# Summing the partial rows of a modulation vector with a ones column, two steps later, in a two-layer hybrid decoder trunk

## Chip, cores, metric

The kernel runs on 1 core of a Trainium2 chip. The metric is device time in microseconds (us) of one execution.

## What is computed

Two layers act on x (512 tokens by 1024). Each layer first makes six modulation vectors of 1024 from the condition c; they scale and shift the two norms and gate the two residual updates. Only the following of the reference matters here:

```python
mod = jax.nn.silu(c) @ ada_w + ada_b                     # (1, 6 * 1024) per layer
sh_m, sc_m, gt_m, sh_f, sc_f, gt_f = jnp.split(mod[:, None, :], 6, axis=-1)
h = rms_norm(x, norm_mix) * (1 + sc_m) + sh_m
...                                                       # input projection and three token mixers
x = x + gt_m * (jnp.concatenate([o_a, o_b, o_c], axis=-1) @ w_out)
h = rms_norm(x, norm_ffn) * (1 + sc_f) + sh_f
gate, up = jnp.split(h @ w_gate_up, 2, axis=-1)
x = x + gt_f * ((jax.nn.silu(gate) * up) @ w_down)
```

## The kernel before, in words

x is kept transposed, as eight tiles `x0` to `x7` of 128 features by 512 tokens. Every large product is taken with both operands split into a high and a low part (`whi`, `wlo` for weights, `hh`, `hl` for the normed activations, `fh`, `fl` for the FFN's), three matmuls for each pair of tiles. `mm` (L298) is the helper that issues every matmul that is not a transpose. In the FFN the products are `pg` (gate), `pu` (up) and `pd` (down); in the mixers `pj`, `pvt` and others. The weights come over SyncE's queue into `wraw` (L570, two buffers, 1 MB each), ScalarE makes the high part (L581), VectorE (sometimes GpSimd) the low part (L582).

The modulation vectors are made by the generator `ada` in halves of 512 columns: 2 layers, 6 vectors, 2 halves, 24 half vectors. The 1024 rows of `ada_w` are eight blocks of 128 partitions. One block is scaled by the column of silu(c) that belongs to it and added to the running sum `acc` of 128 partitions by 512 columns; VectorE does both in one instruction (L413, L415), or ScalarE scales (L417, L420) and GpSimd adds (L418). So when the eight blocks are in, `acc` holds 128 partial rows, and these have to be summed over the partitions, with the result turned from a row of 512 into 4 columns of 128, because `mods[l]` keeps features on partitions.

The end of a half vector does that (L428 and the lines behind it): four transposes of 128 by 128 on TensorE write one PSUM bank `pada` of the two with tag `tp` (L435), VectorE reduces the bank along the free dimension to 4 columns of `mods` (L436) and adds the bias (L437). For the two scale vectors one more small VectorE instruction (L441) makes `na`, the norm's factor.

At the start four half vectors are run one after the other with whole tiles of 4 blocks (the vectors with m of 0 and 1 of layer 0), since the first norm needs them. The other 20 half vectors are side work: `ada` yields after every step of two blocks (tiles `araw2`, which rotate through the three tags `ab0` to `ab2` and show as `araw` in the trace), and the main work calls `next(side)` between its own pieces, in layer 0's mixers (8 half vectors) and in layer 0's FFN (12, those of layer 1). `chain` strings them together; `run` drains a generator.

The order of the instructions on each engine isn't that of the program text: the tile framework schedules the whole program by a timeline of its own, with the priorities that the text sets. A change in one place can so move instructions elsewhere.

Of the kernel before, what the change touches and what calls it, by code (L numbers as in the profile page):

```python
# [227 lines left out]
def trunk(ctx, tc, I, out, dbg=None):  # L228
# [79 lines left out]

    # ---------------- constants and per-layer vectors
    cst = cp.tile([128, CONST_AT["eye16"][0]], F32, name="cst")  # L310
# [50 lines left out]
    V.memset(mhalf, -0.5)  # L361
    V.memset(onesd, 1.0 / D)

    def turn_vrows(l, n=113):
# [12 lines left out]

    # ---------------- modulation: one of the six vectors of a layer
    def ada_raw():
# [4 lines left out]

    pend = [] if "v" in ORDER else [first_vrows]

    def ada(l, m, halves=(0, 1), tile_=ada_raw, eng=G):
        for half in halves:
# [4 lines left out]
            while k < NK:  # L393
                raw = tile_()
                nk = raw.shape[1]
                nc.sync.dma_start(raw, I["ada_w"][l, k * 128:(k + nk) * 128, c0:c0 + 512]
                                  .rearrange("(k p) c -> p k c", p=128))
                for kk in range(nk):
                    t = raw[:, kk]
                    if eng is T:  # L400
                        if k == 0:
                            acc = P("gd", "prow")
                        mm(acc[0:1], scol[:, k:k + 1], t, start=(k == 0), stop=(k == NK - 1))
                        k += 1
                        continue
                    if tile_ is ada_raw:
                        if k == 0:
                            acc = S2("acc")
                        o = acc
                    else:  # L410
                        o = t
                    if eng is V and k:
                        V.scalar_tensor_tensor(o, t, scol[:, k:k + 1], acc, op0=OP.mult, op1=OP.add)  # L413
                    elif eng is V:
                        V.tensor_scalar(o, t, scol[:, 0:1], None, op0=OP.mult)  # L415
                    elif k:
                        A.activation(t, t, AF.Copy, scale=scol[:, k:k + 1])  # L417
                        G.tensor_tensor(o, t, acc, op=OP.add)  # L418
                    else:
                        A.activation(o, t, AF.Copy, scale=scol[:, 0:1])  # L420
                    acc = o
                    k += 1
                if pend:
                    pend.pop()()
                yield
            p = P("tp", "pada")
            if eng is T:
# [5 lines left out]
            else:  # L433
                for j in range(4):
                    T.transpose(p[:, j * 128:j * 128 + 128], acc[:, j * 128:j * 128 + 128], ident)  # L435
                V.tensor_reduce(mods[l][:, c:c + 4], view4(p), axis=AX.X, op=OP.add)  # L436
                V.tensor_add(mods[l][:, c:c + 4], mods[l][:, c:c + 4], vcol[l][:, 16 + c:20 + c])  # L437
            if m in (1, 4):
# [5 lines left out]
    def run(g):  # L444
        for _ in g:
            pass

    # ---------------- norm and split, by halves of the tokens
    HALF = (slice(0, 256), slice(256, 512), slice(0, 512))
# [115 lines left out]
    marks.extend(norm.last)  # L565
    # ---------------- weights: raw pieces and their two parts
    def raw_piece(w, r0, nk, c0, n):
# [43 lines left out]
    def halves(ms, tile_, then, n):  # L611
        for m in ms:
            tile_(0, m)
        after = then(0)
        for j, m in enumerate(ms):
            tile_(1, m)
            for _ in range(n if j else 1):
                next(after, None)
# [7 lines left out]
    def layer(l, side, norm, vt):  # L626
# [8 lines left out]

        # ---- values and gates, token major
        wt = vt if vt is not None else vt_weights(l)
# [15 lines left out]
        if l == 0 and KN["lt"] == 1:  # L653
            with behind(KN["ga"] & 4):
                late()
        # ---- GDN gates
        with prio("gate"):
# [36 lines left out]

        # ---- positions of the compressed blocks
        pe = small("pe", 128, 1)
# [6 lines left out]

        # ---- GDN projections, short convolution
        ckv = {n: c8.tile([128, NH, S], F32, tag=n, name=n) for n in ("ck", "cq", "cv", "cz")}
# [39 lines left out]

        # ---- GDN: norms, token major k
        ck, cq, cv, cz = ckv["ck"], ckv["cq"], ckv["cv"], ckv["cz"]
# [33 lines left out]

        # ---- GDN: decay, (I + A)^T and q k^T of each chunk, keys on partitions
        with prio("dec"):
# [37 lines left out]

        # ---- GDN: inverse of I + A; 32 x 32 blocks in lanes, then two doublings
        with prio("inv"):
# [78 lines left out]

        # ---- GDN: the chunks in turn
        def gdn_out(c):
# [75 lines left out]

        # ---- attention projections
        def rope(p, dst):
# [49 lines left out]

        # ---- compressed keys and values
        w2 = c8.tile([128, 2, 3, 64], F32, tag="w2", name="w2")
# [62 lines left out]

        # ---- attention over keys at or before the query
        def weights_t(pts, nkb):
# [122 lines left out]

        # ---- output projection
        w_out = I["w_out"][l]
# [100 lines left out]
    def chain(*gens):  # L1325
        for g in gens:
            yield from g

    # ---------------- final norm, token major
    def last(norm, i):  # L1330
# [68 lines left out]
```

## Time and profile before

| | |
|---|---|
| median of 3 runs | 1460.61 us (1457.11 to 1462.02) |
| profiled execution, span from first to last instruction | 1460.0 us |
| TensorE matmuls busy, share of the span | 1381.5 us, 95% |
| VectorE busy | 861.2 us, 59% |
| ScalarE busy | 643.6 us, 44% |
| GpSimd busy | 358.9 us, 25% |
| mean granted clock of TensorE, share of full | 0.972 |
| moved from HBM | 168 MB |

The profiled execution shows its span and no other time of its own; the median of the runs is 0.6 us above it. Times in the trace count from the start of the span. The stages follow each other: start to about 60 us, mixers of layer 0 to 392, FFN of layer 0 to 764, mixers of layer 1 to 1092, FFN of layer 1 to the end. A matmul's duration in the trace is its latency, and matmuls overlap: what one costs the stream is the step from its start to the next one's start. Busy PE therefore isn't PE at its peak. PEld is the load of the stationary operand.

### The profile page before, as it was taken

How to read it: one execution, taken by the hardware profiler on the slowest of the kernel's cores; microseconds unless marked ns; L12 is line 12 of the kernel's file. 1: busy time of each engine (PE TensorE's matmuls, PEld its weight loads, DVE VectorE, ACT ScalarE, POOL GpSimd, SP SyncE). 2: the span in 40 equal slices, each digit the busy share in tenths (PEclk: the TensorE clock that was granted, in tenths of full speed). 3: DMA queues.
4: the chain of work that ended last, by engine and by line, in shares of the span. 5: the costliest groups of instructions: out<-in, count | busy, mean ns of one | idle time of the engine just before them, and what ended most of it. 6: DMA issues, size and time to landing. Idle time of an engine off the chain costs nothing.

```text
span 1460.0 us, 21266 instructions
## 1 busy us (share of the span) xinstructions
PE 1381.5 (95%) x8357; PEld 1152.6 (79%) x8357; DVE 861.2 (59%) x1600; ACT 643.6 (44%) x1174; POOL 358.9 (25%) x325
## 2 busy tenths in 40 slices
PE   3789989999999999999999999999999999999997
PEld 3667867787977888788898887778788888888887
DVE  6866877875655555446466576788554343343434
ACT  4567536665543432342254463667443322222231
POOL 4556541344431410140042024124340000000000
PEclk7899999999999999999999999989999999999999
DMA  9646554002056654465441223400212332232231
GB/s 324 220 157 217 152 178 130 4 1 87 30 184 223 193 165 158 131 188 186 125 127 30 87 63 105 145 30 1 82 36 89 101 113 87 87 116 87 87 116 58
DMA packets 137160, 171.47 MB, mean 117 GB/s; under 512 B 14778, under 2 KB 95332, under 8 KB 136932
## 3 DMA queue, kind: packets, MB, share of 16 engines
q1 hardware_dynamic: 137060, 170.11, 36.2%
q8 instruction: 65, 1.06, 0.3%
q14 instruction: 35, 0.29, 0.1%
HBM read 168.00 MB, written 2.10 MB: 117 GB/s over the span
## 4 chain that ended last, share of the span: by engine, by line
PE 78%; DVE 7%; DMA 7%; POOL 3%; ACT 3%; issue 2%; SPq 0%; POOLq 0%; DVEq 0%; ACTq 0%
PE pd L298 16%; PE pg L298 15%; PE pu L298 15%; PE pj L298 11%; DMA araw<-in_ada_w_dram 5%; PE pw L298 3%; PE psc L298 2%; PE pwc L298 2%; PE pob L298 2%; PE ppt L1106 2%; POOL araw L418 2%; PE pvt L298 1%; DVE araw L413 1%; PE pkk L298 1%; DVE wlo L582 1%
## 5 line engine op out<-in xcount | busy, mean ns | idle before, releaser
L581 ACT ACTIVATE whi<-wraw 128x1024 fp32r<-128x1024 f32 (+1 forms) x181 | 187.6, 1038 | 469.2 <-PE pd L298 130.6
L582 DVE TENSOR_TENSOR wlo<-wraw,whi 128x1024 fp32r<-128x1024 f32 (+1 forms) x171 | 218.2, 1276 | 175.3 <-ACT whi L581 169.9
L298 PE MATMUL pj<-hh,whi 128*128 128x512 f32 (+1 forms) x376 | 148.0, 395 | 7.8 <-DVE cacc L714 4.4
L298 PE MATMUL pj<-hh,wlo 128*128 128x512 f32 (+1 forms) x376 | 147.4, 392 | 3.7 <-DVE wlo L582 3.6
L298 PE MATMUL pj<-hl,whi 128*128 128x512 f32 (+1 forms) x376 | 146.6, 390 | 1.0 <-DVE hl L497 1.0
L298 PE MATMUL pg<-hh,whi 128*128 128x512 f32 (+1 forms) x352 | 134.9, 383 | 3.1 <-ACT hh L493 1.8
L298 PE MATMUL pg<-hh,wlo 128*128 128x512 f32 (+1 forms) x352 | 135.3, 384 | 2.7 <-DVE wlo L582 2.7
L298 PE MATMUL pu<-hh,wlo 128*128 128x512 f32 (+1 forms) x352 | 134.9, 383 | 2.0 <-DVE wlo L582 2.0
L298 PE MATMUL pg<-hl,whi 128*128 128x512 f32 (+1 forms) x352 | 134.9, 383 | 0.6 <-DVE hl L497 0.6
L298 PE MATMUL pu<-hh,whi 128*128 128x512 f32 (+1 forms) x352 | 134.1, 381 | 0.3 <-ACT whi L581 0.3
L298 PE MATMUL pu<-hl,whi 128*128 128x512 f32 (+1 forms) x352 | 134.0, 381 | 0.0
L596 DVE SCALAR_TENSOR_TENSOR x<-pd,mods,x 128x512 f32<-128x512 f32 (+1 forms) x112 | 72.6, 671 | 98.0 <-PE pd L298 97.8
L418 POOL TENSOR_TENSOR araw<-araw 128x512 f32<-128x512 f32 x55 | 78.3, 1424 | 162.8 <-ACT araw L417 157.9
L298 PE MATMUL pd<-fl,whi 128*128 128x512 f32 x288 | 112.1, 389 | 0.0
L298 PE MATMUL pd<-fh,whi 128*128 128x512 f32 x288 | 110.0, 390 | 1.0 <-ACT whi L581 1.0
L298 PE MATMUL pd<-fh,wlo 128*128 128x512 f32 x288 | 106.8, 390 | 0.0
L298 PEld LDWEIGHTS pj<-hh,whi 128*128 128x128 f32 x376 | 71.8, 191 | 25.4 <-issue 7.0
L1290 DVE TENSOR_TENSOR sil<-sil,pu 128x512 f32<-128x512 f32 (+1 forms) x48 | 30.8, 641 | 101.3 <-PE pu L298 99.1
L1352 POOL TENSOR_TENSOR fr<-fr,mhalf 128x1 f32<-128x1 f32 x4 | 2.2, 547 | 354.1 <-DVE fr L1351 354.1
L298 PEld LDWEIGHTS pj<-hh,wlo 128*128 128x128 f32 x376 | 71.9, 191 | 19.0 <-DVE wlo L582 5.3
L298 PEld LDWEIGHTS pj<-hl,whi 128*128 128x128 f32 x376 | 71.8, 191 | 13.4 <-DVE hl L497 1.2
L298 PEld LDWEIGHTS pg<-hh,wlo 128*128 128x128 f32 x352 | 66.9, 190 | 16.7 <-DVE wlo L582 4.2
(329 smaller groups left out, 3021.9 us busy)
## 6 DMA issues: line engine op xcount, KB each, us to landing
wraw<-in_w_gate_up_dram SPq DMA_DIRECT2D x44, 1024.0 KB, 5.1
araw<-in_ada_w_dram SPq DMA_DIRECT2D x80, 512.0 KB, 3.9
wraw<-in_w_in_dram SPq DMA_DIRECT2D x22, 1024.0 KB, 5.2
wraw<-in_w_down_dram SPq DMA_DIRECT2D x20, 1024.0 KB, 5.2
araw<-in_ada_w_dram SPq DMA_DIRECT2D x8, 1024.0 KB, 8.3
wraw<-in_w_out_dram SPq DMA_DIRECT2D x8, 1024.0 KB, 5.2
craw<-in_cmp_k_w_dram SPq DMA_DIRECT2D x8, 512.0 KB, 4.0
craw<-in_cmp_v_w_dram SPq DMA_DIRECT2D x8, 512.0 KB, 4.9
```

What stands on the lines that cost most here:

```text
L298: return T.matmul(o, l, r, start=start, stop=stop)
L413: V.scalar_tensor_tensor(o, t, scol[:, k:k + 1], acc, op0=OP.mult, op1=OP.add)
L418: G.tensor_tensor(o, t, acc, op=OP.add)
L581: A.activation(hi, src, AF.Copy)
L582: eng.tensor_tensor(lo, src, hi.bitcast(F32), op=OP.subtract)
L596: V.scalar_tensor_tensor(xt[m][:, sl], p[:, sl], g, xt[m][:, sl], op0=OP.mult, op1=OP.add)
L1106: T.transpose(p[:, (o + kb) * 128:(o + kb) * 128 + 128], pt[:, kb * 128:kb * 128 + 128], ident)
L1290: V.tensor_tensor(s, s, pu[:, sl], op=OP.mult)
L1352: G.tensor_tensor(r, r, mhalf[:, 0:1], op=OP.pow)
```

## The change

The four transposes and the reduction give way to four matmuls, each with a piece of `acc` (128 by 128) as the stationary operand and a column of ones as the moving one; each writes one column of `pada`, so the sum over partitions is already made, and the bias is added straight from PSUM. The tail of `ada` becomes a function `turn_mods`, and is no longer called where a half vector ends: it is put on a list `owed`, and `settle` calls it after the second step of the next half vector (`k == 2 * nk`, two blocks a step), or at the end of `run`, of `chain`, or between the two halves in `halves`. Everything else in the diff is comments taken out, which shifts line numbers (after: L420, L422, L424, L425 for the blocks, L448 for the bias, L298 for the sums).

```diff
     V.memset(onesd, 1.0 / D)
+    ones = cp.tile([128, 1], F32, name="ones")
+    V.memset(ones, 1.0)
...
     pend = [] if "v" in ORDER else [first_vrows]
+    owed = []
+
+    def settle():
+        while owed:
+            owed.pop(0)()
 
     def ada(l, m, halves=(0, 1), tile_=ada_raw, eng=G):
...
                 if pend:
                     pend.pop()()
+                if k == 2 * nk:
+                    settle()
                 yield
+            owed.append(lambda half=half, c=c, acc=acc: turn_mods(l, m, half, c, acc, eng))
+
+    def turn_mods(l, m, half, c, acc, eng):
             p = P("tp", "pada")
...
             else:
                 for j in range(4):
-                    T.transpose(p[:, j * 128:j * 128 + 128], acc[:, j * 128:j * 128 + 128], ident)
-                V.tensor_reduce(mods[l][:, c:c + 4], view4(p), axis=AX.X, op=OP.add)
-                V.tensor_add(mods[l][:, c:c + 4], mods[l][:, c:c + 4], vcol[l][:, 16 + c:20 + c])
+                    mm(p[:, j:j + 1], acc[:, j * 128:j * 128 + 128], ones)
+                V.tensor_add(mods[l][:, c:c + 4], p[:, 0:4], vcol[l][:, 16 + c:20 + c])
...
     def run(g):
         for _ in g:
             pass
+        settle()
...
         after = then(0)
+        settle()
         for j, m in enumerate(ms):
...
     def chain(*gens):
         for g in gens:
             yield from g
+        settle()
```

What it does to the order is shown at three places. The first is VectorE at the start, from the making of `na` of the first half vector to the end of the third. Before:

```order
L441 SCALAR_TENSOR_TENSOR na_92<-mods_90,vcol_88 128x4
L413 SCALAR_TENSOR_TENSOR araw<-araw,scol 128x512
L490 SCALAR_TENSOR_TENSOR ht<-x_132,na_92,pbc 128x512
...
L490 SCALAR_TENSOR_TENSOR ht<-x_135,na_92,pbc 128x512
L413 SCALAR_TENSOR_TENSOR araw<-araw,scol 128x512 x3
L436 TENSOR_REDUCE mods_90<-pada 128x4
L413 SCALAR_TENSOR_TENSOR araw<-araw,scol 128x512
L437 TENSOR_TENSOR mods_90<-mods_90,vcol_88 128x4
L413 SCALAR_TENSOR_TENSOR araw<-araw,scol 128x512
L497 SCALAR_TENSOR_TENSOR hl_277<-ht,mods_90,hh_276 128x512
L436 TENSOR_REDUCE mods_90<-pada 128x4
```

The same stretch with the change (numbers behind names are those of buffers; `hl` is the low part of the normed activations):

```order
L452 SCALAR_TENSOR_TENSOR na_92<-mods_90,vcol_88 128x4
L420 SCALAR_TENSOR_TENSOR araw<-araw,scol 128x512
L502 SCALAR_TENSOR_TENSOR ht<-x_134,na_92,pbc 128x512
...
L502 SCALAR_TENSOR_TENSOR ht<-x_137,na_92,pbc 128x512
L420 SCALAR_TENSOR_TENSOR araw<-araw,scol 128x512 x3
L448 TENSOR_TENSOR mods_90<-pada,vcol_88 128x4
L420 SCALAR_TENSOR_TENSOR araw<-araw,scol 128x512
L509 SCALAR_TENSOR_TENSOR hl_277<-ht,mods_90,hh_276 128x512
L448 TENSOR_TENSOR mods_90<-pada,vcol_88 128x4
```

Between the `ht` group and the first `hl` there stand four accumulating steps instead of five (one went ahead of the group) and no reduction.

The second place is TensorE in the FFN of layer 0, at the last sum of one half vector. Before, the last of the four transposes stands two matmuls into `pu`:

```order
L298 MATMUL pg<-hh_3622,wlo 128x512
L298 MATMUL pu<-hh_3620,whi 128x512
L298 MATMUL pu<-hl_3621,whi 128x512
L435 MATMUL pada<-cst,araw_5037 128x128
L298 MATMUL pu<-hh_3620,wlo 128x512
```

With the change the last sum of that half vector stands behind the whole of that `pu`, 22 matmuls further on:

```order
L298 MATMUL pu<-hh_3612,whi 128x512
L298 MATMUL pu<-hl_3613,whi 128x512
L298 MATMUL pu<-hh_3612,wlo 128x512
L298 MATMUL pada<-ones,araw_5022 128x1
L298 MATMUL pg<-hh_3610,whi 128x512
```

The third is SyncE's queue in the same group of the FFN, where one `araw` load reuses the tile that those sums read, and so waits for them. Before:

```order
L396 DMA araw_5195<-in_ada_w_dram 128x2x512
L570 DMA wraw<-in_w_gate_up_dram 128x8x256 x2
L396 DMA araw_5191<-in_ada_w_dram 128x2x512
L570 DMA wraw<-in_w_gate_up_dram 128x8x256
L396 DMA araw_5273<-in_ada_w_dram 128x2x512
L396 DMA araw_5277<-in_ada_w_dram 128x2x512
L570 DMA wraw<-in_w_gate_up_dram 128x8x256
```

With the change:

```order
L403 DMA araw_5179<-in_ada_w_dram 128x2x512
L582 DMA wraw<-in_w_gate_up_dram 128x8x256 x2
L403 DMA araw_5175<-in_ada_w_dram 128x2x512
L582 DMA wraw<-in_w_gate_up_dram 128x8x256
L403 DMA araw_5250<-in_ada_w_dram 128x2x512
L403 DMA araw_5254<-in_ada_w_dram 128x2x512
```

`araw_5175` is the load that waits for the sums (as `araw_5191` did before); the weight load behind it is the group's fourth here, whereas before the third and the fourth stood behind it.

## Rows read from the trace of the kernel before

**Rows 1.** Windows: length, busy us of PE, PEld, DVE, ACT, POOL, clock, DMA, GB/s.

```profile
0.00:60.00 60.00, 29.54 (x130) 24.15 (x131) 44.47 (x61) 29.50 (x49) 25.56 (x26) 0.77 0.92 303
60.00:392.00 332.00, 310.77 (x2309) 254.62 (x2309) 238.88 (x550) 199.54 (x412) 151.91 (x135) 0.96 0.35 110
392.00:764.00 372.00, 365.86 (x1775) 306.15 (x1775) 201.90 (x259) 135.30 (x191) 78.43 (x60) 1.00 0.52 165
...
21.00:24.20 3.20, 2.86 (x12) 2.46 (x12) 2.15 (x5) 2.46 (x5) 3.04 (x3) 0.50 1.04 386
```

**Rows 2.** Waits of PE at the transposes: line, releaser, us in total, times, longest.

```profile
PE pada L435 <- issue: 9.8, 2, 6.0
PE pada L435 <- POOL araw L418: 4.6, 1, 4.6
```

**Rows 3.** The tile pada: count, ns min/median/max, first and last start, forms.

```profile
L435 PE MATMUL pada<-cst,araw x96: 270/272/477, 23.0 to 713.3; 128*128 128x128 f32 x96
L436 DVE TENSOR_REDUCE mods<-pada x24: 674/684/693, 24.2 to 713.6; 128x4 f32<-128x512 f32 x24
```

**Rows 4.** Timeline of PE, FFN of layer 0: start, us, instruction, count, idle before.

```profile
491.42 0.39 PE L298 MATMUL pg<-hl,whi 128*128 128x512 f32 x1
491.65 0.60 PE L435 MATMUL pada<-cst,araw 128*128 128x128 f32 x4
492.00 0.48 PE L298 MATMUL pg<-hh,wlo 128*128 128x512 f32 x1
492.32 0.40 PE L298 MATMUL pg<-hh,whi 128*128 128x512 f32 x1
...
514.52 0.27 PE L435 MATMUL pada<-cst,araw 128*128 128x128 f32 x1
514.54 0.47 PE L298 MATMUL pg<-hh,wlo 128*128 128x512 f32 x1
```

**Rows 5.** Timeline of PE at a norm's statistic, two one-column sums at full clock.

```profile
756.94 0.28 PE L298 MATMUL pd<-fl,wres 128*128 128x256 f32 x1
757.06 0.50 PE L298 MATMUL pstat<-onesd,ssq 128*128 128x1 f32 x4
757.43 0.36 PE L298 MATMUL pd<-fh,wres 128*128 128x256 f32 x1
757.63 0.28 PE L298 MATMUL pd<-fl,wres 128*128 128x256 f32 x1
```

**Rows 6.** Timeline of PE at the start.

```profile
21.27 1.87 PE L298 MATMUL pstat<-onesd,ssq 128*128 128x1 f32 x8 [4.75 <-DVE ssq L464]
23.01 1.11 PE L435 MATMUL pada<-cst,araw 128*128 128x128 f32 x4
...
40.11 1.09 PE L435 MATMUL pada<-cst,araw 128*128 128x128 f32 x4 [6.05 <-issue]
40.85 0.58 PE L298 MATMUL pvt<-wth,hh 128*128 128x276 f32 x1
...
50.66 1.09 PE L435 MATMUL pada<-cst,araw 128*128 128x128 f32 x4 [3.72 <-issue]
```

**Rows 7.** Timeline of DVE at the start.

```profile
35.70 0.68 DVE L436 TENSOR_REDUCE mods<-pada 128x4 f32<-128x512 f32 x1
36.30 1.81 DVE L413 SCALAR_TENSOR_TENSOR araw<-araw,scol 128x512 f32<-128x512 f32 x1
...
41.24 0.69 DVE L436 TENSOR_REDUCE mods<-pada 128x4 f32<-128x512 f32 x1 [0.56 <-PE pada L435]
```

**Rows 8.** Timeline of PE at three idle gaps that VectorE ended.

```profile
198.82 1.41 PE L1052 MATMUL pcmp<-craw,xw 128*32 128x256 f32 x16 [1.01 <-DVE xw L1048]
...
452.92 0.50 PE L298 MATMUL pu<-hh,wlo 128*128 128x512 f32 x1 [0.82 <-DVE wlo L582]
...
595.03 0.50 PE L298 MATMUL pg<-hh,wlo 128*128 128x512 f32 x1 [1.58 <-DVE wlo L582]
```

**Rows 9.** Waits of SyncE's queue at araw loads: us in total, times, longest.

```profile
SPq L396 <- PE pada L435: 88.0, 13, 14.7
```

## The prediction, made before the changed kernel was run

> **What bounds the kernel now.** I read the page's busy shares first, then the windows by stage, then the waits of TensorE, then its timeline around the instructions that go. The windows [rows 1] show the matmul stream nearly closed: between 60 and 392 us PE is busy 310.8 of 332 us, in the FFN of layer 0 365.9 of 372. So TensorE sets the time everywhere but in the first 60 us (29.5 busy), and a term that lengthens its stream is paid nearly in full, while work taken from VectorE (201.9 of 372 us in that FFN) is worth only what it frees in one of the few gaps. The waits [rows 2] show how much the old transposes held TensorE up: 9.8 + 4.6 us, three waits, the longest 6.0. The timeline shows where: all before 51 us, two of the three among the rows of the start [rows 6]; no later block has an idle time in front of it.
>
> **What goes and what comes on TensorE.** 96 transposes go, 24 blocks of four, the first at 23.0 and the last at 713.3 us [rows 3]. Their price is read from the steps of the stream, not from their durations. At 491.65 a block of four holds the next matmul back by 0.35 us, and that one then keeps the stream for 0.32 us (492.00 to 492.32) where its neighbour took 0.23: 0.35 + 0.09 = 0.44 us, or 0.11 for each transpose. A single one at 514.52 costs the same, 0.02 and the 0.09 behind it [rows 4].
>
> The new sum is a float32 matmul with a 128x128 stationary operand and one moving column. The kernel has that very form already: the norm's statistic `pstat`, two such sums a call. Its rows show four records for the two sums (and eight for two calls), so each float32 sum runs as two passes, each with its own weight load [rows 5, 6]. At the full clock of 2.4 GHz the four records hold the next matmul back 0.37 us, and that one keeps the stream 0.20 instead of 0.12 [rows 5]: 0.45 us, 0.1125 a record. One column streams in no time; what is paid is the load. So a half vector now takes eight records, 0.90 us, instead of 0.44: **+0.46 us**. For the 20 half vectors behind the start that is **+9.2 us**. The bounds: zero if a record hid its load behind a 512-column neighbour as the first of a block does, and 20 x (1.74 - 0.44) = 26 us at the price of the start, where the granted clock is 0.50 (1.2 GHz) [rows 1] and eight such records took 1.74 us (21.27 to 23.01) [rows 6]. I take the row at 2.4 GHz, since the clock in the stages of these sums is 0.96 and 1.00 [rows 1].
>
> Part of it falls into gaps that follow directly. The block at the gap before 198.82 (1.01 us) and the one before 452.92 (0.82 us) have room for 0.46 each [rows 8]: **-0.9 us**. Nothing is left of that if the new order puts the sums elsewhere.
>
> The Trainium skill (page "TensorE: Matmul & The Clock Gate", section "Wait — 56ns, not 53.3ns?") says that start-to-start of small matmuls has a floor of about 25 ns. By that alone eight records would be an estimated 0.2 us and the change would gain on TensorE. The trace disagrees: with the loads counted, a record takes 0.1125 us. The same page's section on LDWEIGHTS, whose estimate for 128 columns is 107 ns, fits the row.
>
> **The start.** The four half vectors there are settled at once by `run`, so nothing is delayed. At 1.2 GHz a block of four costs 0.74 us (40.11 to 40.85) and eight records 1.74: +1.0 us each [rows 6]. The first (23.01) has idle time behind it, and the second is awaited by no matmul that could start; the third and fourth stand directly ahead of matmuls: +2.0 us. Against that, VectorE's chain to the third and the fourth block gets shorter. It loses two reductions, 0.68 + 0.69 us, and one accumulating step, which goes ahead of the `ht` group into a time in which VectorE waits for TensorE; such a step takes up to 1.81 us there [rows 7]; I take 1.3. That is -2.7. Net **-0.7 us**. Ends: +2.0 if another wait takes over at once, -1.2 if the step is worth its 1.81.
>
> **VectorE behind the start.** 20 reductions of 0.684 us go [rows 3], 13.7 us; the addition stays and now reads PSUM. It costs nothing on TensorE's side where the reduction ran beside a closed stream. Where a gap of TensorE is ended by VectorE a reduction ahead in its queue can count. I take **-1.0 us**, one or two of them. Ends: 0, and -11.6 us if all eight in layer 0's mixers count (5.5 us of the 21.2 us that PE idles there) and all 6.1 us of PE's idle time in the FFN go too [rows 1].
>
> **The delay by two steps.** It can gain only where TensorE stood waiting at a transpose, and behind 51 us it never did [rows 2]: 0. The new places aren't even all later; the scheduler deals the sums out singly, up to one whole `pu` apart, and a sum costs two records wherever it stands. The addition behind it follows an instruction that needs the same `pu`, so VectorE's queue waits about as long as before. The bank of `pada` is held longer, but while `pg` and `pu` run, which use other banks. What the delay touches is SyncE's queue: a load of `araw` waits for these sums, with weight loads behind it. Before, that queue waited 88.0 us on `pada` in 13 waits, the longest 14.7 [rows 9], without starving TensorE by more than gaps like the 1.58 us at 595.03 [rows 8]. Price taken: 0; the end is a rival below. The rest of the order (mixers of both layers) moves a little without adding work: 0, give or take 4 us, a fifth of the 21.2 us that PE idles in layer 0's mixers [rows 1].
>
> **Sum.** 9.2 - 0.9 - 0.7 - 1.0 = **+6.6 us**. The profiled execution shows a span of 1460.0 us and the median is 1460.61; on its span the sum gives 1466.6, on the median 1467.2. I predict **1467 us**, slower by 0.4%. About 0.3%, 4.4 us, is what a measurement of this kernel can tell from no change.
>
> **Rivals.** *VectorE was the hidden bound (faster).* If every reduction in the mixers of layer 0 stood on the way to a PE gap (-5.5), the FFN's gaps closed (-6.1) and the start gained its full 1.2, that is -12.8 against +9.2 - 0.9: -4.5, 1456 us. For it: the gaps at 198.82, 452.92 and 595.03 all end with VectorE [rows 8]. Against it: in the FFN VectorE is busy only 54% of the time, and low parts late there were preceded by accumulating steps and waits for ScalarE as much as by reductions. It decides if more than two thirds of those gains arrive. Chance 0.12.
>
> *The records hide their loads (faster).* A transpose set in singly holds its neighbour back by only 0.02 us [rows 4]; if eight records did that, a half vector would cost 8 x 0.02 + 0.09 = 0.25 us, 0.19 less than now: -3.8 for twenty, with the start's -2.7 and VectorE's -1.0 -7.5, 1453 us. The row of `pstat` speaks against it. Chance 0.04. It is what the skill's floor of about 25 ns amounts to.
>
> *The gaps swallow it (no change).* The sums now stand in other places; if the eight of layer 0 all fall beside gaps (21.2 us of them), another 2.8 us go and the start may give its 1.2: about 1464 us. Chance 0.12.
>
> *Late sums hold the weights back (slower still).* The last sum of the half vector shown in the order stands 22 matmuls, at 0.23 us some 5 us, later than the last transpose did, and an `araw` load waits for it with a weight load behind it. If one or two such weight loads become late by that much, PE waits 5 to 10 us more: 1472 to 1477. Against it: fewer weight loads stand behind that wait than before. Chance 0.10.
>
> *The delay does nothing* is part of the forecast, not a case of its own.
>
> **How the numbers follow.** The forecast has the other 0.62, of which I put 0.47 above +4.4 us and 0.15 below, since the sum stands only 2.2 us over the bound and the order's moves are good for 4. Slower: 0.47 + 0.10 = 0.57. Same: 0.15 + 0.12 = 0.27. Faster: 0.12 + 0.04 = 0.16. The range takes in the VectorE rival's 1456 and the lower part of the late weights: 1456 to 1475. The likeliest case alone runs from 1462 to 1472.
>
> **What would show it.** Right: 192 records of `pada` where there were 96; eight of them in a closed stream cost 0.85 to 0.95 us; PE's busy time in the FFN of layer 0 up by 5 to 6 us with idle time about as before; the first `pvt` not more than 3 us from 40.85. Wrong: records stepping by 0.05 us or less; PE's idle time between 60 and 764 us lower by more than 6 us (VectorE was the bound), or higher by 5 with waits on `wlo` or on weight loads (the queue).

## The result, and the profile with the change

The changed kernel took 1472.56 us (median of 4 runs, 1471.63 to 1476.82) beside 1459.75 for the kernel before: a ratio of 1.0089, 95% interval 1.0066 to 1.0111. A second series of the same two kernels gave 1476.77 (5 runs, 1473.86 to 1479.91) beside 1459.77, 1.0111 (1.0092 to 1.0130). The change is slower by 13 to 17 us. The prediction said slower, 1467 us, in a range of 1456 to 1475: the first series lies in it, the second above it.

| | before | with the change |
|---|---|---|
| profiled execution, span | 1460.0 us | 1475.0 us (longest of its four, the others 1469.8 to 1470.8); second series 1478.1 |
| TensorE matmuls busy | 1381.5 us, 8357 records | 1395.0 us, 8453 records |
| VectorE busy | 861.2 us | 847.2 us |
| ScalarE busy | 643.6 us | 638.6 us |
| GpSimd busy | 358.9 us | 361.8 us |
| mean granted clock of TensorE | 0.972 | 0.973 |

The windows of the changed kernel that answer to [rows 1] (length, then busy us of PE, PEld, DVE, ACT, POOL, then granted clock, DMA share, GB/s):

```profile
0.00:60.00 60.00, 33.98 (x143) 29.69 (x144) 43.01 (x58) 32.39 (x53) 29.19 (x29) 0.72 0.92 303
60.00:392.00 332.00, 312.89 (x2310) 256.47 (x2309) 227.23 (x535) 190.15 (x399) 151.73 (x132) 0.96 0.35 110
392.00:764.00 372.00, 361.42 (x1737) 301.61 (x1737) 194.57 (x235) 131.44 (x182) 70.98 (x50) 1.00 0.52 165
```

VectorE lost 11.7 us in the mixers and 7.3 in the FFN; the missing reductions by themselves are 8 x 0.684 = 5.5 and 12 x 0.684 = 8.2, and the windows cut the two kernels at different work. But in the 372 us of the FFN TensorE is busy 361.4 us where it was 365.9, with 1737 records where there were 1775, although it has more to do: it waits.

The tile `pada`, beside [rows 3], and the waits of PE at the sums, beside [rows 2]:

```profile
L298 PE MATMUL pada<-ones,araw x192: 164/250/373, 22.7 to 743.7; 128*128 128x1 f32 x192
L448 DVE TENSOR_TENSOR mods<-pada,vcol x24: 144/154/164, 25.6 to 744.5; 128x4 f32<-128x4 f32 x24
```

```profile
PE pada L298 <- issue: 6.5, 2, 3.4
PE pada L298 <- POOL araw L425: 6.3, 2, 4.6
```

192 records stand where 96 did, and the reduction is gone. A block of eight at full clock, from the timeline of PE in the FFN of layer 0:

```profile
494.06 0.39 PE L298 MATMUL pd<-fh,wlo 128*128 128x512 f32 x1
494.28 0.95 PE L298 MATMUL pada<-ones,araw 128*128 128x1 f32 x8
495.09 0.49 PE L298 MATMUL pg<-hh,whi 128*128 128x512 f32 x1
495.42 0.40 PE L298 MATMUL pg<-hl,whi 128*128 128x512 f32 x1
```

The next matmul starts 0.81 us after the block and keeps the stream for 0.33 where 0.23 is usual: 0.91 us, against 0.44 for four transposes [rows 4]. At the start, the end of the third block, which was at 40.85 [rows 6]:

```profile
38.22 1.84 PE L298 MATMUL pada<-ones,araw 128*128 128x1 f32 x8 [3.41 <-issue]
39.92 0.58 PE L298 MATMUL pvt<-wth,hh 128*128 128x276 f32 x1
```

The first `pvt` comes 0.93 us earlier: the wait of 6.05 us before the block [rows 6] is 3.41 now, with two reductions and a step less on VectorE's way, and the block itself is 1.70 instead of 0.74. By 60 us nothing of that is left: 26 `pj` and 35 `pvt` matmuls have begun (26 and 37 in the second series), 28 and 36 in the kernel before, and the granted clock of these 60 us is 0.72 (0.74) where it was 0.77.

Where the 15 us of the profiled execution went is best read by stages that end at the same instruction: the first gate product `pg` of layer 0, the first `pvt` and the first `pg` of layer 1, the end. Idle is the sum of the idle times before PE's instructions in the FFN of layer 0. The same is listed here for every kernel that was run, in us; the ratio is to the kernel before in the same series:

| kernel | median | ratio to before (95%) | to first `pg` | FFN, layer 0 | idle in it | mixers, layer 1 | FFN, layer 1 |
|---|---|---|---|---|---|---|---|
| before | 1459.8 | | 381.4 | 382.8 | 8.2 | 319.6 | 376.2 |
| changed | 1472.6 | 1.0089 (1.0066 to 1.0111) | 385.0 | 393.7 | 12.4 | 321.7 | 374.7 |
| h, changed again | 1476.8 | 1.0111 (1.0092 to 1.0130) | 387.7 | 392.9 | 11.4 | 322.6 | 374.9 |
| e1 | 1469.3 | 1.0061 (1.0037 to 1.0084) | 384.7 | 383.8 | 5.1 | 323.7 | 376.8 |
| e2 | 1469.9 | 1.0068 (1.0045 to 1.0090) | 381.6 | 390.1 | 15.4 | 320.6 | 374.9 |
| e3 | 1480.0 | 1.0132 (1.0110 to 1.0153) | 379.6 | 399.3 | 8.0 | 318.7 | 376.3 |
| e4 | 1486.7 | 1.0175 (1.0152 to 1.0197) | 399.8 | 387.3 | 6.1 | 325.8 | 376.3 |
| f1 | 1456.2 | 0.9975 (0.9962 to 0.9988) | 381.6 | 379.5 | 8.0 | 318.5 | 376.2 |
| f2 | 1458.7 | 0.9995 (0.9983 to 1.0006) | 381.4 | 381.3 | 7.7 | 316.5 | 376.3 |
| f3 | 1464.9 | 1.0036 (1.0022 to 1.0050) | 383.1 | 384.2 | 6.1 | 321.8 | 378.3 |
| g | 1460.7 | 1.0007 (0.9993 to 1.0021) | 378.9 | 380.6 | 7.8 | 320.5 | 374.7 |
| f5 | 1459.9 | 1.0005 (0.9987 to 1.0024) | 381.6 | 381.9 | 8.2 | 317.2 | 374.7 |
| f6 | 1474.1 | 1.0101 (1.0068 to 1.0133) | 384.9 | 387.5 | 7.2 | 325.2 | 375.0 |
| f7 | 1457.9 | 0.9983 (0.9967 to 0.9999) | 382.7 | 378.9 | 7.1 | 316.7 | 376.2 |

The stages are of one execution each, and executions of one kernel differ by several us (the kernel before by 1453.8 to 1466.2 in 19 runs); a stage that differs by a microsecond or two says nothing by itself. The changed kernel lost 3.7 and 6.4 us up to the first `pg`, **10.8 and 10.1 us in the FFN of layer 0**, 2.0 and 3.0 in the mixers of layer 1, where no half vector is worked on, and gained 1.6 and 1.3 in the last stage.

Of what TensorE itself waits for in the FFN of layer 0 (385.04 to 778.70), these are the two rows that grew most:

```profile
PE pd L298 <- ACT whi L593: 3.0, 2, 1.6
PE pd L298 <- DVE x L608: 2.5, 2, 2.0
```

In the kernel before, the first is 1.0 us and the second is missing, while the largest waits, those for `wlo`, hardly moved: 4.7 us before, 5.0 with the change. ScalarE's own waits in the window 392 to 764 show what comes late:

```profile
ACT araw L424 <- DMA araw<-in_ada_w_dram: 41.8, 16, 4.8
ACT araw L427 <- DMA araw<-in_ada_w_dram: 11.1, 5, 2.9
ACT whi L593 <- DMA wraw<-in_w_down_dram: 6.4, 1, 6.4
ACT whi L593 <- DMA wraw<-in_w_gate_up_dram: 4.8, 1, 4.8
```

In the kernel before the same four were 29.7, 10.8, 2.8 and 14.5 us. So ScalarE waits 12 us more for blocks of `ada_w`, and 6 us less for weights. The total alone is no measure of the harm: over the whole span the wait at L424 is 56.5 us here and 40.9 before, but 51.3 in e1 below, whose FFN is nearly as short as before. ScalarE's queue is in program order, and behind such a wait stands a weight's high part. Two instances, from the timelines of SyncE, ACT, PE and DVE:

```profile
536.50 0.46 SPq L403 DMA_DIRECT2D araw<-in_ada_w_dram  x1
...
544.74 1.33 ACT L424 ACTIVATE araw<-araw,scol 128x512 f32<-128x512 f32 x2 [3.63 <-DMA araw<-in_ada_w_dram]
545.98 1.04 ACT L593 ACTIVATE whi<-wraw 128x1024 fp32r<-128x1024 f32 x1
...
547.08 0.50 PE L298 MATMUL pd<-fh,whi 128*128 128x512 f32 x1 [1.44 <-ACT whi L593]
...
556.13 0.75 DVE L420 SCALAR_TENSOR_TENSOR araw<-araw,scol,araw 128x512 f32<-128x512 f32 x1 [2.24 <-DMA araw<-in_ada_w_dram]
556.80 1.40 DVE L608 SCALAR_TENSOR_TENSOR x<-pd,mods,x 128x512 f32<-128x512 f32 x2
...
557.60 0.50 PE L298 MATMUL pd<-fh,whi 128*128 128x512 f32 x1 [2.04 <-DVE x L608]
```

The load issued at 536.50 is used at 544.74, ScalarE having waited 3.63 us; `whi` stands behind it, and TensorE waits 1.44 for `whi`. At 556.13 VectorE waits 2.24 us for another block; behind it stands the update of `x` that frees the bank of `pd`, and TensorE waits 2.04 for that.

These rows don't yet show late sums behind the late blocks. When the queue came to the load of 536.50 it did not wait for sums: it had stood until 536.04 at a weight load. The load of 550.49, whose block VectorE awaits at 556.13, was released by GpSimd's additions. A load that the sums did hold is the one of 518.06, whose sums ended with two records at 517.75 (SyncE's waits, 511 to 518.5 us):

```profile
SPq L403 <- PE pada L298: 6.6, 1, 6.6
```

The loads follow each other through the same three tiles, so that one late load makes later ones late, but the way from this one to the wait that ends at 544.74 is not shown row by row. What shows the held tile as the cause is the pair e2 and f1 below.

### The profile page after: what moved, and what is told of

The parts are those of the page before. It is cut to its first block, busy times and chain, and to the rows that moved or that the text cites. A ratio compares the mean times of both kernels' runs of the same rounds, so it can differ in the third digit from the quotient of the medians.

```text
span 1475.0 us, 21434 instructions
## 1 busy us (share of the span) xinstructions
PE 1395.0 (95%) x8453; PEld 1166.7 (79%) x8453; DVE 847.2 (57%) x1577; ACT 638.6 (43%) x1170; POOL 361.8 (25%) x325
## 4 chain that ended last, share of the span: by engine, by line
PE 69%; DMA 11%; DVE 7%; POOL 5%; ACT 3%; issue 3%; SPq 1%; POOLq 0%; DVEq 0%; ACTq 0%
PE pd L298 14%; PE pu L298 14%; PE pg L298 14%; PE pj L298 9%; DMA araw<-in_ada_w_dram 9%; POOL araw L425 4%; PE pw L298 3%; PE pwc L298 3%; PE pob L298 2%; PE psc L298 2%; PE ppt L1119 2%; ACT araw L424 1%; DVE wlo L594 1%; SPq L546 1%; PE pvt L298 1%
## 5 line engine op out<-in xcount | busy, mean ns | idle before, releaser
L298 PE MATMUL pj<-hh,whi 128*128 128x512 f32 (+1 forms) x376 | 148.1, 395 | 4.0 <-issue 2.6
L298 PE MATMUL pj<-hh,wlo 128*128 128x512 f32 (+1 forms) x376 | 146.2, 389 | 1.9 <-DVE wlo L594 1.9
L298 PE MATMUL pj<-hl,whi 128*128 128x512 f32 (+1 forms) x376 | 145.9, 388 | 1.0 <-DVE hl L509 1.0
L298 PE MATMUL pg<-hh,whi 128*128 128x512 f32 (+1 forms) x352 | 135.4, 385 | 2.9 <-ACT hh L505 1.8
L298 PE MATMUL pg<-hh,wlo 128*128 128x512 f32 (+1 forms) x352 | 134.9, 383 | 1.6 <-DVE wlo L594 1.6
L298 PE MATMUL pu<-hh,wlo 128*128 128x512 f32 (+1 forms) x352 | 134.6, 382 | 1.5 <-DVE wlo L594 1.4
L298 PE MATMUL pg<-hl,whi 128*128 128x512 f32 (+1 forms) x352 | 134.7, 383 | 0.5 <-DVE hl L509 0.5
L298 PE MATMUL pu<-hh,whi 128*128 128x512 f32 (+1 forms) x352 | 134.1, 381 | 0.0
L298 PE MATMUL pu<-hl,whi 128*128 128x512 f32 (+1 forms) x352 | 133.8, 380 | 0.0
L425 POOL TENSOR_TENSOR araw<-araw 128x512 f32<-128x512 f32 x55 | 77.4, 1408 | 161.3 <-ACT araw L424 158.2
L298 PE MATMUL pd<-fh,whi 128*128 128x512 f32 x288 | 110.6, 392 | 5.5 <-ACT whi L593 3.0
L298 PE MATMUL pd<-fl,whi 128*128 128x512 f32 x288 | 112.2, 390 | 0.0
L298 PE MATMUL pd<-fh,wlo 128*128 128x512 f32 x288 | 107.1, 391 | 2.0 <-DVE wlo L594 2.0
L1303 DVE TENSOR_TENSOR sil<-sil,pu 128x512 f32<-128x512 f32 (+1 forms) x48 | 30.8, 642 | 114.6 <-PE pu L298 112.3
L298 PEld LDWEIGHTS pj<-hh,whi 128*128 128x128 f32 x376 | 71.6, 191 | 18.3 <-issue 2.1
L424 ACT ACTIVATE araw<-araw,scol 128x512 f32<-128x512 f32 x91 | 60.7, 716 | 56.5 <-DMA araw<-in_ada_w_dram 56.5
L298 PEld LDWEIGHTS pj<-hl,whi 128*128 128x128 f32 x376 | 71.7, 191 | 16.2 <-issue 2.8
L298 PEld LDWEIGHTS pj<-hh,wlo 128*128 128x128 f32 x376 | 71.4, 190 | 16.5 <-DVE wlo L594 2.7
```

The source lines that it names most:

```text
L298: return T.matmul(o, l, r, start=start, stop=stop)
L1303: V.tensor_tensor(s, s, pu[:, sl], op=OP.mult)
```

## The experiments

The theories: **A**, the weight-load records of the sums make the loss; **B**, the delay makes it, because the partial rows sit in a tile that a later load of `araw` wants (there are three, and the running sum stays in the last one loaded); **C**, any change of the program reshuffles the scheduler's order and moves the time by some us without a cause of its own. Diffs are against the changed kernel.

**e1, sums at once**

```diff
-            owed.append(lambda half=half, c=c, acc=acc: turn_mods(l, m, half, c, acc, eng))
+            turn_mods(l, m, half, c, acc, eng)
```

> The sums with the ones column stay, the delay goes: `turn_mods` is called where the half vector ends. The orders of TensorE in the start and in the mixers of layer 0 are those of the changed kernel; they part only in the FFN of layer 0. Theory A (the sums' weight-load records, 0.90 us for eight in place of 0.44 us for four transposes, make most of the loss): the time stays near the changed kernel, 1468 to 1473 us, 8 to 12 us over the kernel before. Theory B (the delay makes the loss: the third step's load of `araw` waits for sums that come late, and ScalarE and VectorE then wait for it in front of the weights' parts): the FFN of layer 0 loses its new gaps and the time falls to 1461 to 1465 us. Both halves: about 1467 to 1469.

1469.26 us. The FFN of layer 0 falls from 393.7 to 383.8 us and its idle time from 12.4 to 5.1; the start and the mixers, whose order is the same, stay at 384.7. So the delay costs some 10 us in the FFN and nothing before it, and the sums alone still cost 9.5 us in the whole: both halves of the change lose. The whole fell by 3.3 us against the first series of the changed kernel, less than the FFN did, and by 7.5 against the second.

**e2, transposes delayed**

```diff
-                    mm(p[:, j:j + 1], acc[:, j * 128:j * 128 + 128], ones)
-                V.tensor_add(mods[l][:, c:c + 4], p[:, 0:4], vcol[l][:, 16 + c:20 + c])
+                    T.transpose(p[:, j * 128:j * 128 + 128], acc[:, j * 128:j * 128 + 128], ident)
+                V.tensor_reduce(mods[l][:, c:c + 4], view4(p), axis=AX.X, op=OP.add)
+                V.tensor_add(mods[l][:, c:c + 4], mods[l][:, c:c + 4], vcol[l][:, 16 + c:20 + c])
```

> The delay stays, the four transposes, the reduction and the addition come back. Theory A: 1459 to 1462 us, as before. Theory B: 1464 to 1470 us, with TensorE's idle time in the FFN of layer 0 at 10 us or more against 6.1 before, and ScalarE's waits for the loads of `araw` over 50 us against 40.9. Theory C (any change of the program reshuffles the scheduler's order by several us without a cause of its own): off by 3 us or more in either direction, with the gaps in the mixers and not at the end of the half vectors.

1469.85 us, 10.1 over before: theory B. To the first `pg` it is the kernel before (381.6 and 381.4); the FFN takes 390.1 us, 7.3 more, with 15.4 us idle. The larger part of the added idle time is waits for `wlo`, 9.7 us where the kernel before has 4.7; why these grew is open. The pattern of the changed kernel at 556.13 is here too, from the timelines of DVE and PE:

```profile
546.98 0.75 DVE L420 SCALAR_TENSOR_TENSOR araw<-araw,scol,araw 128x512 f32<-128x512 f32 x1 [2.38 <-DMA araw<-in_ada_w_dram]
547.65 1.40 DVE L609 SCALAR_TENSOR_TENSOR x<-pd,mods,x 128x512 f32<-128x512 f32 x2
...
548.45 0.50 PE L298 MATMUL pd<-fh,whi 128*128 128x512 f32 x1 [2.19 <-DVE x L609]
```

**e3, each sum twice**

```diff
-    V.memset(ones, 1.0)
+    V.memset(ones, 0.5)
...
-                    mm(p[:, j:j + 1], acc[:, j * 128:j * 128 + 128], ones)
+                    mm(p[:, j:j + 1], acc[:, j * 128:j * 128 + 128], ones, stop=False)
+                    mm(p[:, j:j + 1], acc[:, j * 128:j * 128 + 128], ones, start=False)
```

> Each sum is made twice with a column of 0.5 and accumulated in PSUM, so that a half vector takes 16 records instead of 8; all else as in the changed kernel. Theory A, 0.1125 us a record: 20 half vectors behind the start pay 0.90 us more each, 18 us, and the third and fourth at the start up to 1.74 us each: 1488 to 1495 us, 16 to 22 over the changed kernel. Rival (records hide beside their neighbours, the loss is elsewhere): less than 5 us over the changed kernel.

1480.02 us, 7.5 over the first series of the changed kernel, 3.3 over the second: neither. The price of a record is as said, by the timeline of PE:

```profile
431.61 1.84 PE L298 MATMUL pada<-ones,araw 128*128 128x1 f32 x16
433.31 0.49 PE L298 MATMUL pg<-hh,whi 128*128 128x512 f32 x1
433.63 0.40 PE L298 MATMUL pg<-hl,whi 128*128 128x512 f32 x1
```

16 records take 1.70 + 0.09 = 1.79 us, 0.112 each. In the FFN 12 half vectors so owe 10.6 us more; its busy time rose by 10.2 (382.3 to 392.4), its length by 5.7, since 4.4 us of idle time went. Before the first `pg` the time even fell, from 385.0 to 379.6, with TensorE's idle time between the first `pvt` and the first `pg` at 13.9 us instead of 19.8. What was wrong is to take the rest of the order as fixed.

**e4, the partial rows in a tile of their own**

```diff
-                        o = t
+                        o = S2("acc") if k == NK - 1 else t
```

> As the changed kernel, but the last accumulating step of each half vector writes a tile of its own (one of the shared 128x512 slots) instead of the loaded tile, so the delayed sums no longer hold back a load of `araw`. Theory B: the loads of the third step come earlier, ScalarE's waits for the loads of `araw` fall to some 40 us (56.5 in the changed kernel), and the time falls by 3 to 6 us, to 1466 to 1470. Theory A: 1471 to 1474, as the changed kernel. Theory C: off by 3 us or more either way.

1486.69 us, the slowest. The FFN does what theory B says, 387.3 us with 6.1 idle instead of 393.7 with 12.4. But the mixers of layer 0 are 15 us longer: TensorE idles 30.8 us there instead of 19.8. The tile comes out of a set of six that the mixers' working tiles share; whether that is the reason wasn't tried apart. The next runs leave layer 0 alone.

**f1, transposes delayed, own tile in the FFN.** As e2, with `if l and k == NK - 1`.

> As e2_transposes_delayed (transposes and reductions, two steps late), but in the FFN of layer 0 the last accumulating step of each half vector writes a tile of its own, so the late transposes hold no tile that a load wants; the mixers of layer 0 keep the order of the kernel before. Theory B (the held tile is what the delay costs): the FFN of layer 0 falls from 390.1 us to 383 give or take 2, with TensorE idle for 6 to 9 us in it instead of 15.4, and the whole to 1459 to 1463 us. Rival (the delay costs through something else, late additions or the later place of the transposes): the FFN stays at 388 to 392 and the whole at 1466 to 1471.

1456.20 us: beside e2 one tile is changed, and 13.7 us are gone; it is shorter than the kernel before by 0.25%, with 1 outside the interval. The window of the FFN and ScalarE's wait for the blocks over the whole span, in e2:

```profile
381.64:771.76 390.12, 375.80 (x1841) 313.61 (x1842) 215.15 (x276) 141.08 (x207) 82.12 (x65) 1.00 0.50 157
```

```profile
ACT araw L424 <- DMA araw<-in_ada_w_dram: 53.8, 26, 4.4
```

and in f1:

```profile
381.55:761.01 379.46, 372.49 (x1841) 312.98 (x1841) 208.28 (x276) 141.52 (x207) 78.52 (x66) 1.00 0.50 161
```

```profile
ACT araw L424 <- DMA araw<-in_ada_w_dram: 39.1, 22, 3.6
```

The same number of matmuls at a granted clock that reads 1.00 in both, 10.7 us apart, 7.4 of them idle time of TensorE (15.4 and 8.0). In f1 no load of `araw` waits for transposes in this stage; in e2 six do, 44.9 us in all. With transposes the price of the delay in the FFN is the held tile.

**f3, sums only in the FFN, at once.** As e1, with transposes and reduction where `l` is 0.

> No delay; the layer 0 half vectors by transposes and reductions as in the kernel before, only the 12 of the FFN by sums with the ones column. Theory A with what e1_sums_at_once showed: start and mixers of layer 0 as in the kernel before (381 us to the first gate product), the FFN at 383.8 give or take 1.5 (5.5 us of records, most of it given back by gaps that the missing reductions close), the whole 1460 to 1464. Rival (the FFN's gaps closed for another reason, by the shifted order): the FFN at 387 to 389, the full 5.5 us, the whole 1465 to 1467.

1464.90 us, between the two ranges. The FFN is at 384.2, as in e1: the sums add 1.0 and 1.4 us to its length there, with 3.1 and 2.1 us less idle time. That the missing reductions freed it isn't shown: f2 below does without the same reductions, and its idle time is 7.7 us, 8.2 in the kernel before. The rest of the 5.5 us over the kernel before of that series lies outside the FFN, in stages that do the same work; it isn't explained (the profiled execution, 1469.09 us, was the longest of ten).

**f2, fp32r sums in the FFN, at once.** As f3, with

```diff
+    onesr = cp.tile([128, 2], F32R, name="onesr")
+    V.tensor_copy(onesr, ones)
...
-                        o = t
+                        o = S2("accr", F32R) if l and k == NK - 1 else t
...
+                        mm(p[:, 2 * j:2 * j + 2], acc[:, j * 128:j * 128 + 128], onesr)
```

> As f3_sums_at_once_ffn, but the last accumulating step writes the partial rows rounded to fp32r into a tile of its own and the ones column is fp32r with two moving columns, so that a half vector should take four records instead of eight; the partial rows of layer 1's modulation vectors so lose bits. Theory A: 0.45 us a half vector, as the transposes, and no reduction: the FFN at 379 to 382, the whole 1456 to 1460. Rival (the price hangs on the form and not on the number of records): 0.9 us a half vector still, the FFN at 383 to 385, the whole as f3.

1458.67 us, the FFN at 381.3: theory A. Three of the four records, by the timeline of PE:

```profile
638.78 0.39 PE L298 MATMUL pada<-onesr,accr 128*128 128x2 f32 x3
639.03 0.48 PE L298 MATMUL pg<-hh,wlo 128*128 128x512 f32 x1
639.35 0.39 PE L298 MATMUL pg<-hh,whi 128*128 128x512 f32 x1
```

0.25 + 0.09 = 0.34 us for three, 0.113 each: one record for a sum, at the price of a transpose.

**g, f2 with layer 0's sums made twice**

> As f2_fp32r_sums_ffn, but the half vectors of layer 0 are summed twice with a column of 0.5, at once, which gives start and mixers of layer 0 the order that e3_sums_twice had there. Theory C (the order in which the scheduler deals the same work moves the mixers by several us): 379.6 us to the first gate product in spite of 16 records a half vector, as in e3, 1.8 us less than before; with the FFN of f2 the whole is 1453 to 1458. Rival (e3's mixers were short by the chance of that one execution): 388 to 392 us to the first gate product, the price of the added records, and the whole 1463 to 1468.

In the profiled execution 378.9 us to the first `pg`, as e3; but that execution, 1456.5 us, was the shortest of ten, and the median is 1460.70. Over f2 that is 2.0 us for 8 half vectors that owe 8 x (1.79 - 0.44) = 10.8 us more, so most of the price comes back. The whole lies between the two ranges, and whether the order gives it back, as theory C has it, wasn't tried apart. It doesn't beat f2.

**f5, the kernel before with the own tile in the FFN**

> The kernel before with one thing changed: in the FFN of layer 0 the last accumulating step of each half vector writes a tile of its own; transposes and reductions at once. It completes the square of delay and tile (FFN of layer 0: 382.8 us with neither, 390.1 with the delay alone, 379.5 with both). Theory B in its narrow form (only the held tile costs, the delay by itself is worth nothing): the FFN at 379 to 381 and the whole at 1455 to 1458, as f1. Rival (the delay itself helps once the tile is free): the FFN at 382 to 383, the whole at 1459 to 1461.

1459.93 us, the FFN at 381.9: the rival's whole, and its FFN to within 0.1 us. The square in the FFN of layer 0 is so: transposes at once 382.8 and with own tile 381.9; delayed 390.1 and with own tile 379.5. The own tile by itself is worth 1 us, although with it no load of `araw` waits for transposes in the FFN (63.8 us before); with it the delay gains 2.4, without it the delay loses 7.3. The 7.3 is well outside the microsecond or two by which a stage differs anyway; the 2.4 hardly is, but f7 beside f2 shows it again, and the whole of f1 and f5 differs the same way (0.9975 and 1.0005). What it comes from is open, since TensorE's idle time is the same, 8.0 and 8.2 us.

**f6, the changed kernel with the own tile in the FFN**

> The changed kernel with one thing mended: in the FFN of layer 0 the last accumulating step of each half vector writes a tile of its own; sums and delay stay, the mixers of layer 0 keep the order of the changed kernel. Theory B: the FFN falls from 393.7 us to 384 to 387 (f1's 379.5 and up to 5.5 for the records), the whole by 7 to 9 us to 1463 to 1466. Rival (with sums instead of transposes the late loads weren't the cause): the FFN stays at 391 to 394 and the whole at 1470 to 1474.

The FFN falls to 387.5 us, 5.4 to 6.2 less than the changed kernel's two, half a microsecond over the range. The whole does not follow: 1474.08 us, between the two series of the changed kernel, with 325.2 us in the mixers of layer 1. For the kernel with sums it is not shown that mending the tile shortens the whole. Nor does the delay gain there: with the own tile the FFN is still 3.7 us longer than in e1, which has no delay.

**f7, f2 delayed**

> As f2_fp32r_sums_ffn (four records of rounded partial rows in the FFN of layer 0, layer 0's own vectors by transposes), with the sums two steps late as in f1. If the price is the count of records and the tile is free, TensorE pays as much as in f1 and VectorE 12 reductions less: the FFN at 378.5 to 381, the whole at 1454 to 1458. Rival (f1's order, not its freed tile, made it shorter than the kernel before): the FFN at 382 to 385, the whole at 1459 to 1462.

1457.85 us, the FFN at 378.9, the shortest measured. It isn't told apart from f1, so no gain from 12 reductions less on VectorE shows once the tile is free. Beside f2 the delay gains 2.4 us in the FFN.

**h, the changed kernel again**

> The changed kernel once more, unchanged, for a second profiled execution. Its first one was the longest of its four (span 1475.0 us, the others 1469.8 to 1470.8), and f6, which frees the tile in the FFN, was not shorter in the whole than the changed kernel. If the held tile costs the changed kernel 6 to 9 us in every execution, the FFN of layer 0 is again at 391 to 394 us with TensorE idle for 11 us or more, and f6 gave the gain back elsewhere. If the first execution was a long one just there, the FFN is at 387 to 389 with 7 to 9 us idle, and with sums the held tile costs no more than 2 us. The whole: 1470 to 1474 us in either case.

The FFN is at 392.9 us with 11.4 idle: the first execution was no exception there. The median came out above the range, 1476.77.

## Why the prediction was right, and where it was not

- **The number.** The first series, 1472.6, lies in the range, the second, 1476.8, above it. The sum was +6.6 us and the measured change is +12.8 and +17.0; the likeliest case, 1462 to 1472, missed both. The range held the first only because it had taken in the lower part of a rival of chance 0.10, so the direction was right by its reasons, and that the size fell inside is in part luck.
- **The record's price held.** Eight records were put at 0.90 us; they take 0.91, sixteen 1.79, and a single-record form 0.113 each. The rival that records hide their loads is out. The Trainium skill's floor of about 25 ns between small matmuls (page "TensorE: Matmul & The Clock Gate", section "Wait — 56ns, not 53.3ns?") isn't what binds here; the estimate of 107 ns by the same page's section "LDWEIGHTS (loading the stationary operand)" agrees with the measured 0.112 us.
- **What the records cost the whole** was put at +9.2 - 0.9 - 0.7 - 1.0 = 6.6 us with a delay of price 0. e1 is that case, at +9.5, though not by these terms alone: in the FFN the sums cost 1.0 us of length, less than the 5.5 of the records, and 4.1 us came up in the mixers of layer 1.
- **The start** was put at -0.7 us. The first `pvt` does come 0.93 earlier, but by 60 us the changed kernel is no longer ahead, at a granted clock of 0.72 against 0.77; the prediction priced the waits there and not the clock behind them.
- **VectorE behind the start** was put at -1.0 us. In the FFN the idle time fell by 3.1 (e1) and 2.1 (f3) with the reductions gone and the records doubled, but only by 0.5 (f2) with the reductions gone and the price of the transposes kept. So the term isn't refuted, and what closes the gaps in e1 and f3 is open; the longer stream of TensorE, which gives VectorE more time, is a rival that wasn't tried.
- **The delay by two steps, "0", is the step that failed.** It alone costs 10.1 us (e2), and the FFN of the changed kernel is 9.9 us longer than that of e1, which has the sums and no delay. The prediction looked at whether TensorE ever waited at a transpose, and at the bank of `pada`, and named the queue of SyncE as a rival of chance 0.10 at 1472 to 1477 us. That rival has the total and the `araw` loads right. Its path was not right: ScalarE's waits for weight loads fell (17.3 to 11.2 us); what is late is the block of `ada_w` itself, and ScalarE's and VectorE's queues stand still for it with weight parts and updates of `x` behind. Its sign did not come as worded, either. TensorE's idle time between 60 and 764 us rose from 27.4 to 29.7 us, not by 5; in the FFN as a stage it rose from 8.2 to 12.4, at waits for `whi` and `x`, and busy time by 6.5. [Rows 9], 88.0 us of waits on `pada`, gave no warning: with the change that total fell to 59.2 while the harm rose, and e1, whose FFN stays short, has 62.7.
- **The rest of the order, "0 give or take 4"**, was too narrow for an edit in layer 0's mixers. Kernels with the same work there differ by 15 us (e4) and, with more work, by -5 (e3).

The added terms don't sum: sums alone +9.5, delay alone +10.1, both +12.8 and +17.0. In the FFN the cause is shown, by e1, e2, f1 and f6, down to some 4 us that the delayed sums cost even with a tile of their own. Up to the first `pg` the changed kernel is 3.7 us longer, as are e1 and f6 by 3.3 and 3.5; eight half vectors at 0.46 us each would be 3.7. Why the mixers of layer 1 lengthen is open. In the changed kernel one wait there has no releaser, 2.97 in h and 2.26 in e1, and none in the kernel before:

```profile
937.04 0.39 PE L298 MATMUL pj<-hh,whi 128*128 128x512 f32 x1 [2.64 <-issue]
```

## What to carry to other kernels

Price a one-column sum by the records and their weight loads, not by the columns it streams: as float32 it costs twice a transpose of the same block. Before putting off a consumer, ask which buffer its input sits in and which load waits for that buffer: here the same delay of the transposes lost 7.3 us in a stage of 380 with the rows in a rotating load tile and nothing, perhaps a gain of 2.4, with the rows in a tile of their own. Side work in an in-order queue must not wait for its data in front of the main work; the total of a queue's waits does not show that, the instruction behind the wait does.

## What the runs showed of the hardware that was not expected

One wait of TensorE here cost more than its length. In the changed kernel it waits 3.39 us up to 250.23 behind a stretch at full clock, and is then granted half, 1.2 GHz, from the timeline and the windows:

```profile
250.23 0.79 PE L298 MATMUL psc<-akd,aq 64*128 64x128 f32 x2 [3.39 <-DVE mx L1141]
```

```profile
245.00:250.00 5.00, 1.84 (x30) 1.65 (x28) 4.83 (x11) 3.17 (x6) 2.35 (x1) 0.99 0.28 54
250.00:255.00 5.00, 4.77 (x19) 3.67 (x19) 3.85 (x12) 0.60 (x1) 0.00 (x0) 0.50 0.44 167
255.00:260.00 5.00, 4.99 (x32) 4.28 (x32) 3.75 (x11) 3.39 (x8) 0.00 (x0) 0.83 0.01 2
```

In e3, where TensorE has no such wait there (the longest is 0.39 us), the clock stays at 2.4 GHz:

```profile
250.00:255.00 5.00, 4.79 (x26) 3.56 (x26) 4.79 (x14) 2.88 (x5) 1.60 (x1) 1.00 0.17 39
```

By the granted clock of these rows the changed kernel loses 5 x 0.50 + 5 x 0.17 = 3.4 us of full-clock time after a wait of 3.4. The same sum, 5 us times what the granted clock lacks to 1.00, over all windows of 5 us between 40 and 385 us, is 16.1 us in the changed kernel, 8.7 in e3 and 18.4 in e4. So e3's short mixers go with a higher clock. It does not set the changed kernel apart from the kernel before, whose sum is 15.4: there TensorE waits 2.75 us up to 252.56, and the clock is 0.63, 0.50 and 0.84 in the three windows from 250 to 265.
